# Fewer decode steps beside the attention, scans first, shared banks for weights and norms

## The chip, the cores and the metric

The kernel runs on one core of a Trainium2 chip. The metric is the time of one execution on the device in microseconds. Engines: PE (matmuls and weight loads), DVE (vector), ACT (activations), POOL (GpSimd), and SP, whose queue issues all the transfers spoken of here. PE, DVE, ACT and POOL run their instructions in the order in which the program lists them; SP issues its DMAs in program order too.

## The reference

One step of a two-layer decoder for a prompt of 1024 positions and for 8 sample rows with 4096 cached positions each, all float32, model width 1024.

Layer 0 projects the input to q, k, v, two gates and a pooling branch. Eight heads of 64 attend by stick breaking:

```
z = q.k / 8 + bias                       strictly causal
w[t,s] = sigmoid(z[t,s]) * prod over s<j<t of (1 - sigmoid(z[t,j]))
o = w v
```

For the sample rows the keys and values are paged: 32 pages of 128 keys a row, from a pool through a page table. Four groups of the pooling branch take window means. Both branches are gated, projected out, added to a scaled residual and layer-normed. Layer 1 is a convolution module: projection, sigmoid gate, depthwise convolution of 31 taps, layer norm over channels, SiLU, gate, output projection, residual, layer norm.

## The kernel before

A float32 matmul is made of three matmuls of split operands (high part, low part): `project` for the input projections and `out_group` for the output projections, 24 matmuls of 256 columns for a tile of 128 rows and a quarter of the outputs.

The order on PE, ACT, DVE and POOL is the order in which Python calls the engines. Work that is to run beside other work lies in generators: `Filler` advances projection blocks by parts, `tick(n)` advances the sample group's decode by n steps, and `defer`/`point` postpone a function by some points.

*Attention.* 48 units of at most 512 keys: four pairs of heads, eight query blocks, and for the last four blocks two units each, the nearer keys first. An iteration u calls `z_a(u)` (scores in two PSUM banks on PE, then four sigmoids on ACT), `ppart(u-2)` (weights times values on PE), parts of the projections, half of its ticks, `z_b(u)` (for each head a scan and a product on DVE, L365 to L371), more parts, `tpart(u-1)` (PE transposes the weights of both heads into PSUM, L845, ACT copies them to SBUF, L847), the rest of the ticks. How many ticks an iteration has is a running sum of TBASE plus a term in the number of keys. `trp()` hands out PSUM banks in turn, five in this stage, for scores, transposes and whatever else.

*K decode.* A step of `decode_k` loads a pair of pages (two DMAs of 256 KB on SP, L405, into one of four buffers), multiplies the pair that was loaded two steps ago by the query (L417, on POOL or, one time in KMOD, on DVE) and reduces the pair before that over the head dimension (L409 on DVE). Two halves of four rows have 64 pairs each; behind each half come transposes, sigmoids, a scan over the keys and products, in ten steps. Steps that are left when the attention ends run in the first output projection, one for each of its 32 groups, and in the first parts of the next stage.

*Output projections.* `out_layer` goes through 32 groups (four quarters, eight tiles of 128 rows). Behind each group DVE adds the residual (L1062) and takes statistics (L1066). When a tile has all quarters, `norm_s` makes mean and rs (DVE, POOL) and a deferred function applies the norm: a first pass on DVE, (y - mean) x gamma (L1009 with gamma in PSUM, in halves, L1013 with gamma in SBUF), a second one, y x rs + beta, on DVE for the tiles in FAST (L1018), else on ACT (L1020) and POOL (L1021). The first projection has gamma in two PSUM banks, the second not. In the second every other group's accumulator is a `trp()` bank, of which that stage has four.

*Between.* The convolution stage runs projections on PE, taps on DVE, ACT and POOL, the V decode and the sample path in ticks. Then `mid_a` spreads the norm's mean and rs of a chunk of tiles over partitions (transposes L1555, L1556, into a `trp()` bank of which that stage has two), `mid_b` applies them on DVE (L1567), and SiLU, gate and split follow, before the second output projection.

Of the kernel before, what the change touches and what calls it, by code (L numbers as in the profile page):

```python
# [14 lines left out]
F32 = mybir.dt.float32  # L15
# [3 lines left out]
AF = mybir.ActivationFunctionType  # L19
# [5 lines left out]
P = 128  # L25
D = 1024
S = 1024
# [18 lines left out]
KS = 30  # L46
PS_ = 15
NEG = -1e30
KMOD = 8
KPOOL = 7  # L50
ENG = mybir.EngineType
KLAG = 2
DTB = 2
# [12 lines left out]
WRB = 3  # L66
ETICK = 0.35
EDVE = (1, 2, 3, 0)
TBASE = 2.8
TSLOPE = 1.5  # L70
NHEADS = (0, 6, 6, 6, 6, 6, 6, 6)
SNY = 7
# [12 lines left out]
SNZ = 5  # L85
HALVES = (3, 6)
OLAG = 3
FAST = (5, 6, 7)
WCONVA = ((0, 5), (1, 5))
SY = 2  # L90
VRATE = 1.575
# [9 lines left out]
def kernel(  # L101
# [44 lines left out]
    def trp():  # L146
        return pz[0].tile([P, 512], F32, tag="zt", name="zt", bufs=NZT[0])
# [323 lines left out]
    def tick(n):  # L471
        while n > 0 and queue:
            try:
                next(queue[0])
                n -= 1
            except StopIteration:
                queue.pop(0)
# [359 lines left out]
    def tpart(u):  # L837
        pair, qb, c0, c1, first, last = units[u]
        n = c1 - c0
        wts = []  # L840
        for hh in range(2):
            w = st["w", u, hh]
            t = trp()
            for i in range(n // P):
                pe.transpose(out=t[:, i * P:(i + 1) * P], in_=w[:, i * P:(i + 1) * P], identity=ident)  # L845
            wt = ab.tile([P, 512], F32, tag="wt", name="wt", bufs=3)
            act.activation(out=wt[:, 0:n], in_=t[:, 0:n], func=AF.Copy)  # L847
            wts.append(wt)
        st["t", u] = wts
# [97 lines left out]
    for u in range(len(units) + 2):  # L947
        if u < len(units):
            pair, qb, c0, c1, first, last = units[u]
            n = c1 - c0  # L950
            if u % 12 == 0:
                fill.until(f"v{pair}")
                fleft = 42 if pair < 3 else 45
                fbase = fleft / 12.0
            fcred += fbase
            tcred += TBASE + TSLOPE * (384 - n) / 384.0
            z_a(u)
        k = int(tcred)
        tcred -= k
        f = min(int(fcred), fleft)  # L960
        fcred -= f
        fleft -= f
        fs = [(f + 2 - i) // 3 for i in range(3)]

        def slot(i):
            if i == PAT and u > 1:
                ppart(u - 2)
            if i == TAT and 0 < u <= len(units):
                tpart(u - 1)

        slot(0)
        fill.part(fs[0])
        tick((k + 1) // 2)
        if u < len(units):
            z_b(u)
        slot(1)
        fill.part(fs[1])
        slot(2)
        tick(k // 2)
        fill.part(fs[2])  # L980
        slot(3)
# [23 lines left out]
    def norm_a(gb, y, mv, halves, gps):  # L1005
        if gps:
            for i in range(2):
                h = slice(i * 512, i * 512 + 512)
                dve.scalar_tensor_tensor(out=y[:, h], in0=y[:, h], scalar=mv[:, 0:1], in1=gps[i],  # L1009
                                         op0=ALU.subtract, op1=ALU.mult)  # L1010
            return
        for h in halves:
            dve.scalar_tensor_tensor(out=y[:, h], in0=y[:, h], scalar=mv[:, 0:1], in1=gb[:, 0, h],  # L1013
                                     op0=ALU.subtract, op1=ALU.mult)

    def norm_b(gb, y, rs, fast, h):
        if fast:
# [15 lines left out]
    def out_layer(w, first, ahead, X, gb, pool, finish, between, before=None, half=None, tail=None, lag=OLAG, fast0=FAST, wide=0, gps=()):  # L1033
# [16 lines left out]
        for s, (n4, tb) in enumerate(order):  # L1050
# [16 lines left out]
            if n4 == 3:  # L1067
                fast = tb in fast0
                halves = (slice(0, 512), slice(512, 1024)) if tb >= 6 else (slice(0, 1024),)
                mv, rs = norm_s(pool, sts[tb])  # L1070

                def app(y=y, mv=mv, rs=rs, tb=tb, fast=fast, halves=halves):
                    norm_a(gb[0], y, mv, halves, gps)
                    for h in halves:
                        norm_b(gb[0], y, rs, fast, h)
                        finish(tb, y, h)
                defer((DTC if fast0 is FASTB else DTD)[tb], app)
# [472 lines left out]

    def mid_a(c):
        a, b = MID[c]
        t = trp()
        for i, tb in enumerate(range(a, b)):
            pe.transpose(out=t[:, i * P:(i + 1) * P], in_=rmf[:, tb:tb + 1].broadcast_to([P, P]), identity=ident)  # L1555
            pe.transpose(out=t[:, 256 + i * P:256 + (i + 1) * P], in_=rvf[:, tb:tb + 1].broadcast_to([P, P]),  # L1556
                         identity=ident)
        BC[c] = t
# [37 lines left out]
            X[tb] = C[:, tb].rearrange("p k c -> p (k c)")  # L1596
            sp.dma_start(X[tb], x1_dram[tb * P:(tb + 1) * P, :])

    gb1 = [None]

    def before(n4, tb):
        if (n4, tb) in STEPS:
            STEPS[n4, tb]()
        if n4:
            return
        if tb == 3:
            gb1[0] = G[:, 0:2].rearrange("p t k c -> p t (k c)")
            sp.dma_start(gb1[0][:, 0, :], ln_c_g.to_broadcast([P, D]))
            sp.dma_start(gb1[0][:, 1, :], ln_c_b.to_broadcast([P, D]))
# [22 lines left out]
    mid_c(0)  # L1632
    mid_g(1)
    flush()
    swap_psum("pzd", 4)
    cxp.close()
    dx = ctx.enter_context(tc.tile_pool(name="dx", bufs=1, reuse_waits="tile"))
    fill.part(2)
# [14 lines left out]
    mid_g(2)  # L1653
    flush()
    deep[0] = DEEPD
    out_layer(w_out1, first1, ahead1, X, gb1, dx, fin1, lambda n4, tb: tick(1), before, lambda: tick(1))
    while queue:
        tick(1)
    flush()
# [24 lines left out]
```

## Time and profile before

| | |
|---|---|
| median of 3 runs | 1143.98 us (1140.2 to 1145.24) |
| profiled execution | 1143.3 us, span 1141.5 us |
| granted clock, mean | 0.971 |
| PE busy | 1051.7 us, 92% |
| DVE busy | 812.6 us, 71% |
| POOL busy | 665.1 us, 58% |
| ACT busy | 491.9 us, 43% |

The page also cuts the span into 40 equal slices of 28.5 us; a digit is the busy share in tenths:

```profile
PE   8998888889999998797998999999999999899994
DVE  3458878688599898767348399999999960484246
POOL 3277879691788889872418336765766612343235
DMA  8577767783467976655203887787687678386922
```

The attention is about the fourth to the eighteenth slice, the first output projection the nineteenth to the twenty-second, the convolution stage follows up to the thirty-fourth, and the second output projection has the last five.

### The profile page before, as it was taken

The page shows a single profiled execution, that of the slowest core. Times are in us where ns is not written, and L with a number is a line of the kernel's source. Part 1 is how long each engine was busy: PE and PEld are TensorE (multiplying, and loading weights), DVE is VectorE, ACT ScalarE, POOL GpSimd, SP SyncE. Part 2 cuts the span into 40 slices and gives each one's busy share as a digit, 9 for nine tenths or more (in the row PEclk, how much of TensorE's full clock was granted, in tenths as well). Part 3 has the DMA queues.
Part 4 walks back from the last instruction along what each step waited for, and adds up shares of the span by engine and source line. Part 5 has one row for each costly group of instructions (what it writes and reads, how often), then busy time and mean ns, then how long its engine had stood idle before and what let it go on. Part 6 is the DMA issues. An engine that isn't in the chain of part 4 may idle for free.

```text
span 1141.5 us, 19830 instructions
## 1 busy us (share of the span) xinstructions
PE 1051.7 (92%) x6804; PEld 841.7 (74%) x6804; DVE 812.6 (71%) x961; ACT 491.9 (43%) x929; POOL 665.1 (58%) x502
## 2 busy tenths in 40 slices
PE   8998888889999998797998999999999999899994
PEld 7897777768877877697997666566666466677784
DVE  3458878688599898767348399999999960484246
ACT  4345465547565565571204224444544422462210
POOL 3277879691788889872418336765766612343235
PEclk9999999999999999898999999999999999899997
DMA  8577767783467976655203887787687678386922
GB/s 267 170 230 231 243 194 222 207 251 98 141 217 219 278 216 216 199 194 203 68 26 142 240 253 249 234 252 217 194 266 236 210 237 264 122 280 218 322 102 113
DMA packets 179206, 235.20 MB, mean 206 GB/s; under 512 B 15418, under 2 KB 95939, under 8 KB 179081
## 3 DMA queue, kind: packets, MB, share of 16 engines
q1 hardware_dynamic: 179105, 233.94, 65.1%
q8 instruction: 53, 0.87, 0.3%
q14 instruction: 48, 0.39, 0.1%
HBM read 212.60 MB, written 16.14 MB: 200 GB/s over the span
## 4 chain that ended last, share of the span: by engine, by line
PE 54%; POOL 13%; DVE 11%; issue 9%; DMA 7%; ACT 3%; SPq 3%; POOLq 0%; DVEq 0%; ACTq 0%
PE acc L225 11%; PE acc L227 10%; PE acc L226 10%; POOL kt L417 7%; PE qv L1151 5%; DMA kt<-in_cache_k_dram 3%; DVE zw L409 3%; PE acc L1029 3%; POOL wlo L210 2%; PE acc L1031 2%; PE acc L1030 2%; DVE kp L365 2%; DMA vt<-in_cache_v_dram 1%; DVE xl L196 1%; POOL xres L1021 1%
## 5 line engine op out<-in xcount | busy, mean ns | idle before, releaser
L225 PE MATMUL acc<-xh,whi 128*128 128x384 f32 (+2 forms) x960 | 361.5, 377 | 11.5 <-DVE hbt L705 5.7
L227 PE MATMUL acc<-xl,whi 128*128 128x384 f32 (+2 forms) x960 | 340.4, 355 | 0.2 <-DVE xl L196 0.2
L226 PE MATMUL acc<-xh,wlo 128*128 128x384 f32 (+2 forms) x960 | 339.7, 354 | 0.0
L417 POOL TENSOR_TENSOR kt<-kt,qbs 128x1024 f32<-128x1024 f32 x112 | 274.1, 2464 | 39.6 <-DMA kt<-in_cache_k_dram 30.0
L210 POOL TENSOR_TENSOR wlo<-wraw,whi 128x512 fp32r<-128x512 f32 x122 | 161.6, 1328 | 184.1 <-ACT whi L205 179.5
L1373 DVE SCALAR_TENSOR_TENSOR conv_acc<-hbuf,wdwT,conv_acc 128x1024 f32<-128x1024 f32 x196 | 252.8, 1290 | 6.8
L225 PEld LDWEIGHTS acc<-xh,whi 128*128 128x128 f32 x960 | 184.3, 192 | 78.1 <-issue 26.1
L409 DVE TENSOR_REDUCE zw<-kt 128x16 f32<-128x1024 f32 x128 | 153.6, 1212 | 63.5 <-POOL kt L417 63.3
L227 PEld LDWEIGHTS acc<-xl,whi 128*128 128x128 f32 x960 | 184.3, 192 | 18.0 <-DVE xl L196 0.7
L226 PEld LDWEIGHTS acc<-xh,wlo 128*128 128x128 f32 x960 | 185.0, 193 | 15.7 <-issue 0.3
L1363 POOL TENSOR_TENSOR conv<-conv,tap 128x512 f32<-128x512 f32 x84 | 105.9, 1293 | 17.6 <-ACT tap L1360 17.6
L1029 PE MATMUL acc<-whi,xh 128*128 128x256 f32 x352 | 102.4, 291 | 0.0
L1031 PE MATMUL acc<-whi,xl 128*128 128x256 f32 x352 | 99.5, 283 | 2.1 <-DVE xl L196 2.1
L1030 PE MATMUL acc<-wlo,xh 128*128 128x256 f32 x352 | 99.4, 282 | 0.0
L365 DVE TENSOR_TENSOR_SCAN kp<-kp,zt 128x512 f32<-128x512 f32 (+3 forms) x96 | 92.4, 963 | 1.2 <-ACT zt L361 1.2
L205 ACT ACTIVATE whi<-wraw 128x512 fp32r<-128x512 f32 x126 | 77.4, 624 | 32.1 <-DMA wraw<-in_w_out_ab_dram 14.1
L360 ACT ACTIVATE kp<-zt,nbiash 128x512 f32<-128x512 f32 (+3 forms) x96 | 55.8, 581 | 71.4 <-DVE sg L371 40.7
L1360 ACT ACTIVATE tap<-hbuf,wdwT 128x512 f32<-128x512 f32 x84 | 59.7, 721 | 48.0 <-POOL conv L1363 38.1
L1151 PE MATMUL qv<-vt,zw 128*32 128x512 f32 x512 | 76.1, 604 | 3.1 <-DMA vt<-in_cache_v_dram 3.1
L1029 PEld LDWEIGHTS acc<-whi,xh 128*128 128x128 f32 x352 | 66.8, 190 | 7.9 <-issue 7.4
L1031 PEld LDWEIGHTS acc<-whi,xl 128*128 128x128 f32 x352 | 67.0, 190 | 2.3 <-DVE xl L196 2.3
L845 PE MATMUL zt<-ident,sg 128*128 128x128 f32 x288 | 44.7, 286 | 24.2 <-DVE sg L371 12.9
(274 smaller groups left out, 1507.3 us busy)
## 6 DMA issues: line engine op xcount, KB each, us to landing
kt<-in_cache_k_dram SPq DMA_DIRECT2D x256, 256.0 KB
vt<-in_cache_v_dram SPq DMA_DIRECT2D x256, 256.0 KB
wraw<-in_w_in_c_dram SPq DMA_DIRECT2D x48, 256.0 KB
vt<-in_w_in_c_dram SPq DMA_DIRECT2D x48, 256.0 KB
wraw<-in_w_in_ab_dram SPq DMA_DIRECT2D x46, 256.0 KB
xt<-in_x_prompt_dram SPq DMA_DIRECT2D x8, 512.0 KB
wraw<-in_w_out_ab_dram SPq DMA_DIRECT2D x16, 256.0 KB
xres<-in_x_prompt_dram SPq DMA_DIRECT2D x8, 512.0 KB
```

What stands on the lines that cost most here:

```text
L210: (eng or gp).tensor_tensor(out=lo, in0=raw, in1=hi.bitcast(F32), op=ALU.subtract)
L225: pe.matmul(o, hi[:, k % 4, :], xh, start=(k == 0), stop=False)
L226: pe.matmul(o, lo[:, k % 4, :], xh, start=False, stop=False)
L227: pe.matmul(o, hi[:, k % 4, :], xl, start=False, stop=(k == NK - 1))
L365: dve.tensor_tensor_scan(out=kr, data0=kr, data1=z[:, 0:1].broadcast_to([P, n]), initial=1.0 if prev is None else prev, op0=ALU.mult, op1= ...
L409: dve.tensor_reduce(out=seg[:, j // 8, j % 8:j % 8 + 2, bi * 8:bi * 8 + 8], in_=kts.pop(s - KLAG - 1).rearrange("p a (h d) -> p a h d", d=DH),
L417: eng.tensor_tensor(out=kt, in0=kt, in1=qrow[b], op=ALU.mult)
L1029: pe.matmul(o, XH[:, k, cs], hi[:, k % 2, :], start=(k == 0), stop=False)
L1030: pe.matmul(o, XH[:, k, cs], lo[:, k % 2, :], start=False, stop=False)
L1031: pe.matmul(o, XL[:, k, cs], hi[:, k % 2, :], start=False, stop=(k == NK - 1))
L1151: pe.matmul(pv[32 * bi:32 * bi + 32, :], Z[:, j % 8 * 4 + j // 8, :], vts[bi], start=(j == 0), stop=(j == NPG - 1), tile_position=(0, 32 * ...
L1373: dve.scalar_tensor_tensor(out=part[1], in0=hb[:, j:j + S], scalar=w, in1=part[1], op0=ALU.mult, op1=ALU.add)
```

## The change

TBASE goes from 2.8 to 2.35, KMOD and KPOOL from 8 and 7 to 4 and 3, FAST loses tile 6. In the attention's loop `z_b(u)` is called ahead of the first ticks. Units of at most 256 keys put the transposes of both heads into one bank and copy them at once. A fast tile in a layer that has gamma in PSUM takes `norm_fast`: the first pass writes into a `trp()` bank, the second reads it; the second projection now gets gamma in PSUM too. That layer's `trp()` banks go from four to three. `mid_a` puts the first two chunks into the bank pair that held the convolution's accumulator.

```
-KMOD = 8
-KPOOL = 7
+KMOD = 4
+KPOOL = 3
-TBASE = 2.8
+TBASE = 2.35
-FAST = (5, 6, 7)
+FAST = (5, 7)
 def tpart(u):
+        if n <= 256:
+            t = trp()
+            for hh in range(2):
+                for i in range(n // P):
+                    pe.transpose(out=t[:, hh * 256 + i * P:hh * 256 + (i + 1) * P],
+                                 in_=st["w", u, hh][:, i * P:(i + 1) * P], identity=ident)
+            wt = ab.tile([P, 512], F32, tag="wt", name="wt", bufs=3).rearrange("p (a n) -> p a n", a=2)
+            act.activation(out=wt[:, :, 0:n], in_=t.rearrange("p (a n) -> p a n", a=2)[:, :, 0:n], func=AF.Copy)
+            st["t", u] = [wt[:, 0], wt[:, 1]]
+            return
...
         fill.part(fs[0])
-        tick((k + 1) // 2)
         if u < len(units):
             z_b(u)
+        tick((k + 1) // 2)
...
+    def norm_fast(gb, y, mv, rs, h, i, gps):
+        t = trp()
+        dve.scalar_tensor_tensor(out=t, in0=y[:, h], scalar=mv[:, 0:1], in1=gps[i], op0=ALU.subtract, op1=ALU.mult)
+        return lambda: dve.scalar_tensor_tensor(out=y[:, h], in0=t, scalar=rs, in1=gb[:, 1, h], op0=ALU.mult, op1=ALU.add)
...
+                    if fast and gps:
+                        hs = (slice(0, 512), slice(512, 1024))
+                        bs = [norm_fast(gb[0], y, mv, rs, h, i, gps) for i, h in enumerate(hs)]
+                        for h, b in zip(hs, bs):
+                            b()
+                            finish(tb, y, h)
+                        return
...
 def mid_a(c):
-        t = trp()
+        if c == 0:
+            BC["wide"] = pz[0].tile([P, S], F32, tag="conv", name="rows", bufs=1)
+        t = BC["wide"][:, c * 512:c * 512 + 512] if c < 2 else trp()
...
+        if (n4, tb) == (2, 4):
+            gps1.extend((psum("o", 1), pg.tile([P, 512], F32, name="scale1")))
+            for i in range(2):
+                act.activation(out=gps1[i], in_=gb1[0][:, 0, i * 512:i * 512 + 512], func=AF.Copy)
...
-    swap_psum("pzd", 4)
+    swap_psum("pzd", 3)
+    pg = ctx.enter_context(tc.tile_pool(name="pg", bufs=1, space=PSUM, reuse_waits="tile"))
```

## Rows read from the trace of the kernel before

**Rows 1.** Stretches: busy us (count) of PE, PEld, DVE, ACT, POOL; PEclk, DMA share, GB/s
```profile
80.00:503.00 423.00, 376.92 (x2576) 326.73 (x2575) 336.68 (x408) 236.34 (x490) 328.43 (x182) 0.96 0.68 210
...
536.00:588.00 52.00, 52.00 (x441) 51.83 (x440) 18.64 (x39) 7.83 (x16) 11.99 (x11) 1.00 0.14 42
588.00:640.00 52.00, 47.80 (x329) 41.81 (x327) 32.54 (x59) 20.39 (x32) 33.43 (x45) 1.00 0.44 147
...
1127.00:1141.50 14.50, 0.21 (x2) 0.01 (x1) 9.85 (x15) 0.85 (x1) 6.84 (x6) 0.61 0.37 145
```

**Rows 2.** Waits of PE, 80 to 503 us: us in total, times, longest
```profile
PE zt L845 <- DVE sg L371: 12.9, 7, 3.2
PE zt L845 <- DVE sg L369: 10.8, 10, 2.4
PE acc L225 <- DVE hbt L705: 5.7, 4, 2.3
```

**Rows 3.** Waits of DVE, 80 to 503 us
```profile
DVE zw L409 <- POOL kt L417: 57.1, 31, 5.4
...
DVE kp L365 <- ACT zt L361: 1.2, 1, 1.2
```

**Rows 4.** Timeline of DVE: start us, us, instruction, [idle before <-releaser]
```profile
227.72 1.22 DVE L409 TENSOR_REDUCE zw<-kt 128x16 f32<-128x1024 f32 x1 [2.63 <-POOL kt L417]
...
231.20 1.27 DVE L365 TENSOR_TENSOR_SCAN kp<-kp,zt 128x512 f32<-128x512 f32 x1
```

**Rows 5.** Timeline of PE, the same stretch
```profile
233.39 0.66 PE L845 MATMUL zt<-ident,sg 128*128 128x128 f32 x4 [2.60 <-DVE sg L371]
```

**Rows 6.** DVE by form, 80 to 503 us: busy us, mean ns, idle before
```profile
L409 DVE TENSOR_REDUCE zw<-kt 128x16 f32<-128x1024 f32 x118 | 141.7, 1212 | 57.4 <-POOL kt L417 57.1
...
L417 DVE TENSOR_TENSOR kt<-kt,qbs 128x1024 f32<-128x1024 f32 x15 | 26.9, 1792 | 0.0
...
L437 DVE TENSOR_TENSOR_SCAN kpd<-kpd 128x1024 f32<-128x1024 f32 x1 | 2.3, 2279 | 0.0
```

**Rows 7.** POOL by form, 80 to 503 us
```profile
L417 POOL TENSOR_TENSOR kt<-kt,qbs 128x1024 f32<-128x1024 f32 x104 | 254.4, 2464 | 39.3 <-DMA kt<-in_cache_k_dram 29.7 <-DVE kp L365 3.9 <-DVE zw L409 3.2
L210 POOL TENSOR_TENSOR wlo<-wraw,whi 128x512 fp32r<-128x512 f32 x43 | 56.6, 1318 | 26.7 <-ACT whi L205 26.7
```

**Rows 8.** Line 417, the whole span: ns min/median/max, first and last start us
```profile
L417 DVE TENSOR_TENSOR kt<-kt,qbs x16: 1209/1276/3224, 79.5 to 524.8; 128x1024 f32<-128x1024 f32 x16
```

**Rows 9.** ACT by form, 80 to 503 us
```profile
L847 ACT ACTIVATE wt<-zt 128x512 f32<-128x512 f32 x48 | 26.4, 601 | 14.9 <-PE zt L845 14.8
...
L847 ACT ACTIVATE wt<-zt 128x256 f32<-128x256 f32 x16 | 5.4, 385 | 2.6 <-PE zt L845 2.6
```

**Rows 10.** Timeline of DVE in the first output projection, one group
```profile
564.42 0.42 DVE L1062 SCALAR_TENSOR_TENSOR xres<-xres,acc 128x256 f32<-128x256 f32 x1 [1.96 <-PE acc L1031]
564.88 0.43 DVE L1066 BATCH_NORM_STATS2 st<-xres 128x6 f32<-128x256 f32 x1
```

**Rows 11.** Timelines of PE and of POOL before the second output projection
```profile
987.79 0.45 PE L1555 MATMUL zt<-ident,rmu 128*128 128x128 f32 x1 [5.68 <-DVE conv L1567]
...
993.26 0.69 POOL L1243 COPY sB<-shs 128x64 f32<-128x64 f32 x1
```

**Rows 12.** Timeline of DVE at the end
```profile
1122.67 3.58 DVE L1013 SCALAR_TENSOR_TENSOR conv<-conv,mv,gate 128x1024 f32<-128x1024 f32 x2
1127.53 1.28 DVE L1018 SCALAR_TENSOR_TENSOR conv<-conv,rs,gate 128x1024 f32<-128x1024 f32 x1 [1.29 <-POOL rs L1002]
...
1129.94 2.29 DVE L1013 SCALAR_TENSOR_TENSOR conv<-conv,mv,gate 128x512 f32<-128x512 f32 x2
...
1137.09 1.41 DVE L1018 SCALAR_TENSOR_TENSOR conv<-conv,rs,gate 128x512 f32<-128x512 f32 x2 [0.45 <-POOL rs L1002]
```

**Rows 13.** Groups by line over the whole span, with gamma in PSUM
```profile
L1009 DVE SCALAR_TENSOR_TENSOR xres<-xres,mv,qv 128x512 f32<-128x512 f32 x8 | 5.9, 740 | 0.0
...
L1018 DVE SCALAR_TENSOR_TENSOR xres<-xres,rs,lngb 128x512 f32<-128x512 f32 x2 | 3.2, 1626 | 0.0
```

**Rows 14.** Chain of waits: start us, us, what
```profile
150.35 4.79 DMA kt<-in_cache_k_dram
```

More of the change, by code (lines that the diff above doesn't have):

```diff
@@ L1597, in mid_c @@
             sp.dma_start(X[tb], x1_dram[tb * P:(tb + 1) * P, :])
-    gb1 = [None]
+    gb1, gps1 = [None], []
     def before(n4, tb):
@@ L1655 @@
     deep[0] = DEEPD
-    out_layer(w_out1, first1, ahead1, X, gb1, dx, fin1, lambda n4, tb: tick(1), before, lambda: tick(1))
+    out_layer(w_out1, first1, ahead1, X, gb1, dx, fin1, lambda n4, tb: tick(1), before, lambda: tick(1), gps=gps1)
     while queue:
```

## The prediction, before the run

> **What bounds the kernel now.** I read the table of stretches first [rows 1]: its PE column says where the tensor engine stands idle and its clock column where it runs at 1.2 instead of 2.4 GHz. Of the 1141.5 us span, 80 to 503 us is the attention loop with the K pages of the sample group decoded beside it. PE is busy there for 376.9 of 423 us, 46 us idle, and the granted clock averages 0.96. The output projection after it (536 to 588 us) has PE busy throughout while DVE works 18.6 and POOL 12.0 of 52 us, and DMA moves only 42 GB/s. So the idle tensor time is in the attention, and the spare vector, POOL and DMA time lies right behind it.
>
> Who keeps PE waiting is in the waits of PE [rows 2]: transposes of the attention weights (L845) that wait for the last vector step of those weights (12.9 and 10.8 us), and projection groups that wait for DVE to empty an accumulator (5.7 us). Always DVE. What DVE itself waits for is POOL: 57.1 us before the page reduction L409, against 1.2 us for the sigmoids its scans need [rows 3]. One stretch of DVE's timeline shows the mechanism [rows 4]: a reduction waits 2.63 us for POOL's product, and the scan of the next weights comes only behind it and another reduction; PE's transposes of those weights then start after 2.60 us of idling [rows 5]. DVE runs in order, so a wait for POOL is a wait of everything behind it. Busy time plus waits for POOL is 336.7 + 57.1 = 394 of DVE's 423 us: with its waits DVE, not PE, sets the pace here. POOL in turn is busy for 328.4 us and waits some 30 us for pages and 27 us for weights [rows 7].
>
> **The change part by part.** The sum is made against the profiled execution, 1143.3 us (span plus 1.8), which is 0.7 us under the median of the runs.
>
> *Fewer K steps in the attention (TBASE 2.8 to 2.35).* Counted from the code: the loop over 48 units issues 48 x TBASE steps of the K decode (the term in n sums to zero), 134 before and 112 after, behind 8 steps issued earlier. The decode has 155. So 13 steps are left for the projection before, 35 after: 22 pages' pairs (two DMAs, one product, one reduction each) leave the attention. *Products three of four on POOL instead of seven of eight (KMOD, KPOOL).* Up to the end of the attention DVE now makes 26 of 104 products instead of 15 of 126, POOL 78 instead of 111.
>
> DVE in the attention: 22 reductions less at 1.212 us, -26.7; 11 products more at 1.792 us, +19.7 [rows 6]; busy 336.7 - 7.0 = 329.7 us. POOL: 33 products less at 2.464 us, -81 us, 328 to 247 [rows 7]. What remains of DVE's 57.1 us of waits for POOL no row shows. Below it is 0 (POOL has 40% of its time free), above 57.1 (nothing changes). I take half, 28.5: the lateness that comes from POOL's own load should go, that which comes from the landing of pages stays, since the rate of page loads per us hardly changes. DVE's other idle time, 423 - 336.7 - 57.1 = 29.2, I keep. 329.7 + 28.5 + 29.2 = 387.4: -36 us. The ends: with all waits kept 416, -7; with none kept 359, and then PE is the bound: by the clock column some 34 of its 423 us ran at half speed, which at full speed would take 17 less of its 376.9 busy us, so 360, -63.
>
> A price for DVE's product that speaks against this stands in its own row: 1.209 us at least, 1.276 in the median, 3.224 at most [rows 8]. At 3.224 us for all 26 the attention gains 37 us less: 26 x 3.224 - 26.9 is +57 instead of +19.7; at 1.276 it gains 13 more. I stay at the mean, which holds both kinds. The Trainium skill, GPSIMD Engine Reference, section Key points, says that POOL shares its SBUF interfaces with VectorE and contends with DVE instructions that have two SBUF inputs. These products have two, so by that rule the long price is to be expected whenever POOL works beside them, and the attention would gain next to nothing. The trace agrees in part: rows 8 have the long price, but half of the products took 1.276 us or less while POOL was busy for 328 of 423 us.
>
> *Scans ahead of the steps.* Nothing is added or removed; z_b moves past one or two steps of each iteration, and past nothing on SP or POOL. The weights are then ready before DVE can be caught behind POOL. What it adds is the wait of a scan for PE and the sigmoids of the same iteration, with the reductions queued behind it, and behind those SP's page loads that wait for free buffers. In rows 3 that wait is 1.2 us in all because DVE is late; it only grows when DVE is early, when it costs nothing. I count it inside the 28.5 us.
>
> *One bank and one copy for units of up to 256 keys.* 16 of 48 units. In half of them two copies of 385 ns become one like the 601 ns form [rows 9], 0.17 us less; the smaller half saves as much: 16 x 0.17 = 2.7 us on ACT, which is busy for 236 of 423 us [rows 1]. Both heads now wait for the later one, but the products that read them come an iteration later. Zero, at most +1; the freed bank may take a little off too.
>
> *The 22 pairs in the output projection.* A group there takes 2.84 us: DVE's 0.42 and 0.43, then 1.96 us idle for PE [rows 10]. A step adds 1.212 + 1.792/4 = 1.66, so DVE has 2.5 of 2.84 us (2.87 with every product at 3.224). POOL gets 0.75 x 2.464 = 1.85 us a group, and 3.15 in the eight groups with a 1.318 us weight split, 2.5 us too much in all; pages are requested three groups before their reduction. DMA goes from 42 to some 210 GB/s, what the attention has [rows 1]. Hidden in the main, but the residual rows and weights are loaded on the same SP queue: I take +4, from 0 to +12 (half a microsecond a group). Behind it the end of the decode, with a scan of 2.279 us on DVE [rows 6], falls into the normalisation (588 to 640 us, DVE 32.5 of 52 busy): +2, 0 to +5. The last tile's two second passes there took 1.626 us each; like the first ones with a PSUM operand they should take about 0.74 [rows 13]: 1.8 us less, of which I count -1, 0 to -2.
>
> *Broadcast rows of the convolution's norm in a bank of their own.* PE waits 5.68 us here [rows 11] because the third broadcast needs the bank of the second, which DVE reads late. That wait goes. But the next thing on PE after two parts of a projection is the sample product, and its operand is copied on POOL at 993.26 [rows 11], behind work that hangs on the same DVE chain and not on this bank. PE would be there as much earlier and wait. 0, from -6 to +1; the one bank fewer for the last projection I price within it.
>
> *The tail.* PE ends at about 1127 us [rows 1], and DVE works off norms until 1138.5, the end of the last row [rows 12]. A step of 1024 takes 1.28 us there, but two others take 3.58; two halves take 1.41 or 2.29. With gamma in PSUM a half costs 0.74 [rows 13], so a tile's first pass is 1.48. Tiles 5 and 7 go through four such steps, tile 6 gives its second pass (1.41 us) to ACT and POOL, and the waits of 1.29 us for rs shrink since DVE no longer sits on it between. Laid out from 1122.67: tile 4's first pass ends at 1124.2, tile 5's at 1125.6 and its second at 1127.1, instead of 1128.8. Tile 6 adds its last sum and statistics (1.15) and a first pass: 1129.8. The same for tile 7: 1132.4. Its rs comes on POOL behind tile 6's two halves of 1.2, which start at 1130.5 behind ACT's 0.6: 1132.9, and 0.8 for rs. The second pass then ends at 1135.2 instead of 1138.5. -3, from -5 (no wait for rs) to +1 (POOL's halves as much stretched as DVE's).
>
> Sum: -36 + 4 + 2 - 1 + 0 - 3 = -34 us: 1109.
>
> **Rivals.**
> *The waits for POOL stay (1130).* POOL's products wait for pages 29.7 us [rows 7], and steps still come in pairs, so a reduction asks for a product issued just before it. Then the attention gains its 7 us of work and a few of the order, say 15, and with the other terms 1143.3 - 15 + 4 + 1 - 3 = 1130. For it: DMA is at 0.68 share before and after. Against it: pages are three steps ahead, and 81 us of POOL work go.
>
> *PE becomes the bound (1085).* Scans first and a POOL at under two thirds leave nothing late; attention -58 (5 above its floor), the rest as above: 1143.3 - 58 + 2 - 2 = 1085. For it: all four large waits in rows 2 are behind DVE. Against: DVE would have to be busy for 330 of 365 us without catching on anything.
>
> *The projection gives it back (1157).* Place: groups 0 to 23 of the first output projection. A page buffer comes free with a reduction on DVE and is used again four units on; between lie the landing, POOL's product behind a weight split, and the reduction: 2.46 + 1.32 + 1.21 = 5.0 us plus the landing, for four groups. A slow landing took 4.79 us [rows 14], so 9.8 us for four groups, 2.45 each, under the 2.84 of PE. If residuals, weights and pages together bring the landing to 15 us, a group takes 5.0 us, 24 of them cost 52 us more, and the sum is 1109 - 4 + 52 = 1157. It begins to cost from a landing of 6.4 us and eats all (38 us) from 12.7. Against it: some 210 GB/s are asked, which the attention has all the time.
>
> *It does not do what it says (1145).* DVE is as late as before, since its own work falls by 7 us only and products at the long price of rows 8 eat that and the shorter waits: -36 + 37 in the attention, + 4 + 1 - 3 behind it: 1146, or 1145 with one of them short. POOL is then faster and nobody gains by it. The page named at rows 8 stands for this one.
>
> **How the numbers follow.** Forecast 1109 (0.60, own range 1094 to 1122); waits stay 1130 (0.17); PE the bound 1085 (0.11); gives it back 1157 (0.05); nothing 1145 (0.07). The range 1086 to 1136 leaves out the two cases at the top and half of the lowest. Under 0.5%, 5.7 us, a change of this kernel can't be told from none. Faster by more: 0.60 + 0.17 + 0.11 = 0.88; within: 0.07; slower: 0.05.
>
> **What would show it.** Right: between the start and the end of the attention PE idles for under 25 us, DVE's waits for POOL before L409 fall to around 28 us and come behind the scans, L845's waits for DVE fall from 23 us to a few; L409 and L417 run on into the normalisation, with projection groups still 2.84 us apart; PE idle before L1555 is gone and stands before the sample product; the last DVE step comes 3 us sooner after the last matmul. Wrong: groups over 3 us apart with DVE waiting for POOL; DVE's products mostly at 3 us; PE in the attention idle as long as before.

## The result, and the profile after

The changed kernel takes 1112.17 us (median of 4 runs, 1107.29 to 1117.8) against 1144.59 us of the kernel before in the same comparison: ratio 0.9726, 95% interval 0.9673 to 0.978, faster. The forecast was 1109. The execution that was profiled took 1107.29 us, of which 1105.5 are the span. Its span is 36.0 us shorter than that of the profile before, near the forecast's 34, but the gain does not lie in the same places.

The busy times of the page after:

```profile
PE 1040.4 (94%) x6804; PEld 837.7 (76%) x6804; DVE 830.9 (75%) x982; ACT 493.1 (45%) x917; POOL 628.8 (57%) x488
```

The table of stretches after, with the columns of [rows 1]: the attention, the middle of the first output projection, its end with the start of the convolution stage, and the tail:

```profile
80.00:465.00 385.00, 370.00 (x2611) 326.75 (x2611) 329.36 (x402) 238.71 (x482) 259.38 (x153) 0.98 0.68 206
...
493.00:545.00 52.00, 46.90 (x392) 46.28 (x391) 40.81 (x53) 6.06 (x10) 41.14 (x21) 1.00 0.75 247
545.00:608.00 63.00, 53.27 (x352) 47.28 (x354) 38.96 (x66) 24.63 (x39) 36.01 (x50) 0.95 0.35 122
...
1095.00:1105.50 10.50, 0.00 (x0) 0.00 (x0) 6.05 (x12) 1.33 (x2) 5.15 (x7) 0.64 0.52 201
```

PE idles 15 us in the attention, where it idled 46. In the first projection's middle DVE and POOL, which had most of that time free before, are busy for 41 of 52 us, and PE, which had been busy throughout, now idles 5. The third line is new trouble: PE idles 10 of 63 us there.

To see where time is won and lost, the same instructions are looked up in PE's timeline of each trace. Times in us, and the lead that a kernel has over the kernel before at that point:

```
                                      before   after   lead   lead:    lead:   lead: decode earlier
                                                              steps    order   and norm in SBUF
                                                              alone    alone   (see below)
first matmul, first out-projection     507.2   465.7   41.5    38.4     13.8    40.5
last matmul of that projection         614.7   576.4   38.3    25.3     14.0    33.0
last transposes of its normalised rows 632.0   600.7   31.3    17.8     14.1    31.3
PE's last matmul                      1127.2  1094.7   32.5    16.6     13.5    32.8
end of the span                       1141.5  1105.5   36.0    16.7     13.1    36.3
```

(Of the kernel after the fastest execution was profiled, of the steps alone the slowest of four and of the last column's kernel the slowest of five, so that the first and the last column of leads end alike where the medians differ by 8 us; and one execution of the order alone, the 1141.57 us below, fell into a slower state and is not in its ratio.) The attention wins 41.5 us (36 forecast), the projection and the start of the convolution stage give back 10.2 (5 forecast), 1.2 more come up to PE's last matmul, and the tail wins 3.5 (3 forecast).

The two longest waits of PE in the attention after, columns as in [rows 2]:

```profile
PE zt L713 <- DVE hbt L705: 3.7, 1, 3.7
PE zt L815 <- issue: 2.8, 2, 1.7
```

The two large waits of [rows 2], the transposes of the weights behind DVE's last weight steps, were 23.7 us and are not among these. And what DVE waits for, beside [rows 3]:

```profile
DVE zw L409 <- POOL kt L417: 18.3, 16, 3.7
DVE qo L756 <- ACT sga_t L754: 8.9, 1, 8.9
DVE kp L365 <- ACT zt L361: 6.1, 5, 2.5
```

57.1 us of waits for POOL are 18.3 now, and the scans' wait for the sigmoids grew from 1.2 to 6.1 us, as the prediction said that it would when DVE is early. The 8.9 us before L756, a step of the setup, were as long before.

### The profile page after: what moved, and what is told of

Read it like the earlier page. It is cut to its first block, busy times and chain, and to the rows that moved or that the text cites. A ratio compares the mean times of both kernels' runs of the same rounds, so it can differ in the third digit from the quotient of the medians.

```text
span 1105.5 us, 19839 instructions
## 1 busy us (share of the span) xinstructions
PE 1040.4 (94%) x6804; PEld 837.7 (76%) x6804; DVE 830.9 (75%) x982; ACT 493.1 (45%) x917; POOL 628.8 (57%) x488
## 4 chain that ended last, share of the span: by engine, by line
PE 52%; DVE 8%; DMA 5%; POOL 4%; ACT 3%; issue 2%; SPq 1%; POOLq 0%; DVEq 0%; ACTq 0%
PE acc L225 11%; PE acc L227 10%; PE acc L226 10%; PE qv L1173 6%; DMA kt<-in_cache_k_dram 2%; DVE conv L1591 2%; POOL kt L417 2%; PE acc L1044 2%; PE zt L1044 1%; PE qv L1209 1%; PE o L871 1%; PE acc L1046 1%; PE acc L1045 1%; PE zt L1046 1%; PE zt L1045 1%
## 5 line engine op out<-in xcount | busy, mean ns | idle before, releaser
L417 POOL TENSOR_TENSOR kt<-kt,qbs 128x1024 f32<-128x1024 f32 x96 | 235.7, 2466 | 77.0 <-DMA kt<-in_cache_k_dram 61.7
L1045 PEld LDWEIGHTS acc<-wlo,xh 128*128 128x128 f32 x352 | 67.2, 191 | 1.1 <-POOL wlo L210 1.1
```

The lines of the kernel that those rows point to most:

```text
L417: eng.tensor_tensor(out=kt, in0=kt, in1=qrow[b], op=ALU.mult)
L1045: pe.matmul(o, XH[:, k, cs], lo[:, k % 2, :], start=False, stop=False)
```

## The experiments

Each experiment has its own median and a ratio to the kernel before, run on the same chip in turns with it. The kernel before had medians of 1142.56, 1140.9 and 1143.89 us in the three sets (the first four experiments, the next four, the last four), and the kernel after ran in a set of its own: between sets the ratios compare better than the medians.

**The parts of the attention alone.** Two theories: *W*, that the fewer steps bring the gain, as in the prediction's sum; *O*, that the order of scans and steps does. Four kernels: the kernel before with one part each, and the kernel after with one part taken back.

```diff
-TBASE = 2.8
+TBASE = 2.35
```

> The kernel before with TBASE 2.35 alone: 22 pairs of pages leave the attention, order and shares stay. Theory W (the work on DVE and its waits for POOL set the pace of the attention): DVE does 22 reductions and 3 products less, 336.7 - 32 = 305 us, waits for POOL half of 57, so PE is the bound and the attention is 40 to 45 us shorter; 10 to 15 us are given back up to the convolution stage, where the decode now ends; no gain at the tail: about 1144 - 42 + 13 = 1115. Theory O (the order scans behind steps makes PE wait, and the order alone cures it): attention at most 10 us shorter, the same given back: 1144 to 1150.

Measured: 1120.08 us (1118.25 to 1126.64), ratio 0.9801 (0.9773 to 0.9829).

```diff
-        tick((k + 1) // 2)
         if u < len(units):
             z_b(u)
+        tick((k + 1) // 2)
```

> The kernel before with z_b ahead of the first steps and nothing else. Theory W: DVE has the same work and waits for POOL, so it is as late as before: attention 0 to 8 us shorter, 1136 to 1144. Theory O: the scans no longer stand behind reductions that wait for POOL, the 23 us that L845 waits for DVE go and part of the rest: 1112 to 1120.

Measured: 1129.79 us (1123.09 to 1141.57), ratio 0.986 (0.9817 to 0.9904).

```diff
-KMOD = 8
-KPOOL = 7
+KMOD = 4
+KPOOL = 3
```

> The kernel before with three of four products on POOL instead of seven of eight and nothing else. Theory W: DVE takes 16 more products in the attention, +29 us at 1.79, POOL loses 39 us, DVE's waits for POOL fall by about 29: 1140 to 1148. Rival P (POOL alone is the bound, DVE's waits follow its load at once): waits fall from 57 to under 15 and DVE's products are short: 1125 to 1132. Theory O: no change, 1144.

Measured: 1151.28 us (1149.63 to 1153.27), ratio 1.0083 (1.0056 to 1.011).

The fourth is the kernel after with the order of before (the second diff backwards):

> The changed kernel with z_b again behind the first steps. Theory W: the order is worth little once DVE has time left: 0 to 6 us over the changed kernel, 1112 to 1118. Theory O: the 23 us come back: 1132 to 1138.

Measured: 1117.88 us (1116.68 to 1120.07), ratio 0.9787 (0.976 to 0.9814).

The same stretch of each, 80 to 460 us, and DVE's waits for POOL in it. The kernel before:

```profile
80.00:460.00 380.00, 341.44 (x2335) 295.46 (x2335) 309.05 (x377) 212.99 (x451) 294.38 (x165) 0.97 0.69 211
DVE zw L409 <- POOL kt L417: 51.1, 28, 5.4
```

Fewer steps alone:

```profile
80.00:460.00 380.00, 360.68 (x2550) 314.96 (x2549) 304.97 (x383) 233.74 (x487) 275.05 (x160) 0.99 0.67 205
DVE zw L409 <- POOL kt L417: 40.6, 24, 3.4
```

The order alone:

```profile
80.00:460.00 380.00, 345.71 (x2374) 300.97 (x2373) 318.60 (x388) 215.58 (x456) 299.24 (x167) 0.97 0.71 216
DVE zw L409 <- POOL kt L417: 36.1, 31, 5.5
```

The share alone:

```profile
80.00:460.00 380.00, 337.84 (x2279) 292.00 (x2277) 327.24 (x388) 206.76 (x441) 261.87 (x148) 0.95 0.69 208
DVE zw L409 <- POOL kt L417: 32.4, 20, 5.4
```

The kernel after with the order of before:

```profile
80.00:460.00 380.00, 359.70 (x2545) 313.31 (x2544) 321.99 (x398) 232.80 (x470) 251.38 (x147) 0.99 0.68 206
```

The numbers in brackets behind PE count its matmuls: how far a kernel gets in the same time. With fewer steps 2550, with the share alone 2279. Fewer steps make the attention 38 us shorter, just under W's 40 to 45; 21 us of that are lost again behind it in the profiled execution (the table of leads), and by the medians the whole is 22 us shorter. The order alone makes the attention 14 us shorter and loses nothing, which is more than W allowed and half of what O asked. What it takes away is seen in the waits; PE's for DVE with the order alone:

```profile
PE acc L225 <- DVE hbt L705: 7.9, 5, 2.6
PE acc L225 <- DVE kl L611: 6.0, 2, 3.3
PE zt L845 <- DVE sg L371: 5.2, 6, 1.4
```

L845's waits, 22.5 us in this stretch of the kernel before, fall to 5.4 with as many steps as before; DVE still waits 36.1 us for POOL, and projections still wait for the accumulator (13.9 us, 11.2 before). In the kernel after the order is worth 5.7 us by the medians and 7 by the ratios, with intervals that overlap; its attention is 4 us longer without it, longer than in any of the six profiled runs that have the attention of the kernel after. So the order and the steps take away the same waits, and their gains don't add: 38 and 14 alone, 41.5 together.

The share alone costs 8.7 us: DVE gets 18 us of work more, and its waits for POOL fall by 18.7, so that DVE is as late as before and L845's waits stay (22.7 us). I had expected a loss of at most half of 8.7 us.

Two sums can be held against PE's idle time in these 380 us. By the waits for POOL alone, the kernels would stand in another order: 51.1 us in the kernel before, 40.6 with fewer steps, 36.1 with the order, 32.4 with the share, where PE idles 38.6, 19.3, 34.3 and 42.2 us. DVE's busy time plus these waits is 360.2, 345.6, 354.7 and 359.6 us: it sets fewer steps first and the order second, as PE's idle time does, and leaves the kernel before and the share alone last and alike.

**The share taken back in the kernel after.**

```diff
-KMOD = 4
-KPOOL = 3
+KMOD = 8
+KPOOL = 7
```

> The kernel after with POOL making 7 of 8 products again instead of 3 of 4. About 14 products of the attention go from DVE (1.6 us each, 22 us less on DVE) to POOL (2.45 us each, 34 us more, 290 of 385). Theory S (DVE's busy time sets the attention once the steps are fewer, as the share alone cost 9 us in the kernel before): DVE's waits for POOL grow by less than 12 us and the attention is 5 to 10 us shorter, 1102 to 1107. Theory P (the share and the fewer steps are needed together, POOL's lateness comes back): DVE's waits for POOL grow by over 22 us and it takes 1115 to 1125.

Measured: 1111.53 us (1109.89 to 1116.37), ratio 0.9741 (0.9713 to 0.9768). It is the same time, between what the two theories asked; the waits grew by less than 12 us, as S had it, but nothing was gained by it. The stretch of the attention, beside the first line of the table after:

```profile
80.00:465.00 385.00, 371.30 (x2610) 328.85 (x2610) 306.49 (x388) 238.32 (x482) 282.03 (x164) 0.97 0.67 205
```

DVE has 23 us less to do and POOL 23 more, and PE stands where it stood, busy for 371 instead of 370 of 385 us. DVE's waits for POOL are 24.5 us instead of 18.3, and its waits for ACT's copies grow (L794 from 4.7 to 8.6 us, L611 to 6.4). With 2.35 steps a unit, neither the work of DVE nor that of POOL sets the attention's end any more; PE is within 14 us of it. The share, which was one of the sum's terms (+19.7 us on DVE), is worth nothing in the kernel after.

**One bank and one copy taken back.**

```diff
-        if n <= 256:
+        if False:
```

> The kernel after with each head's transposed weights in a bank and a copy of its own again, also for units of at most 256 keys. ACT gets about 2.7 us of copies back in the attention, of 236 busy in 385 us. If ACT and the banks have slack, as the prediction has it: within 2 us of the kernel after, 1110 to 1114. If the bank that the shared copy saves is what lets PE run ahead: PE waits for zt banks grow and the attention is 5 to 10 us longer, 1117 to 1122.

Measured: 1112.42 us (1104.34 to 1116.16), ratio 0.9744 (0.9713 to 0.9776). No difference, as the sum had it.

**The tail taken back.**

```diff
-FAST = (5, 7)
+FAST = (5, 6, 7)
...
-        if (n4, tb) == (2, 4):
-            gps1.extend((psum("o", 1), pg.tile([P, 512], F32, name="scale1")))
-            for i in range(2):
-                act.activation(out=gps1[i], in_=gb1[0][:, 0, i * 512:i * 512 + 512], func=AF.Copy)
...
-    swap_psum("pzd", 3)
+    swap_psum("pzd", 4)
```

(and the last projection called without gamma's copies)

> The kernel after with the last normalisation of before: gamma from SBUF, tile 6 on the fast path, four banks instead of three in the last projection. If the tail's gain is what the rows at the end show: the span's last part is 3 to 4 us longer and nothing else moves, 1115 to 1116. If the bank given up costs as much in the last projection as the norm gains: 1111 to 1113, with the projection's last matmul earlier.

Measured: 1114.81 us (1114.48 to 1117.91), ratio 0.9772 (0.9745 to 0.9798). From PE's last matmul to the end of the span it takes 14.3 us, as before the change; the kernel after takes 10.8. The last projection itself is as long with four banks as with three (127.7 and 128.4 us from its first matmul to its last). The intervals of the whole overlap; the 3.5 us rest on the traces alone.

**Where the gain is given back.** Between the last projection group and the last transposes of the normalised rows the kernel after loses 7.0 us. PE's timeline of the kernel after there; in square brackets the idle time before the instruction:

```profile
582.79 0.23 PE L451 MATMUL zt<-ident,crow 1*128 1x1 f32 x1 [2.49 <-DVE xl L196]
...
585.68 1.19 PE L1148 MATMUL zt<-ident,xres 128*128 128x128 f32 x8
589.60 1.97 PE L463 MATMUL zt<-ident,zw 128*128 128x128 f32 x8 [2.73 <-DVE xl L196]
```

and DVE's, up to the step that released PE at 589.60:

```profile
583.88 0.75 DVE L1028 SCALAR_TENSOR_TENSOR zt<-xres,mv,o 128x512 f32<-128x512 f32 x1
584.53 0.75 DVE L1028 SCALAR_TENSOR_TENSOR zt<-xres,mv,qv 128x512 f32<-128x512 f32 x1
585.30 1.41 DVE L1029 SCALAR_TENSOR_TENSOR xres<-zt,rs,lngb 128x512 f32<-128x512 f32 x2
586.63 2.20 DVE L454 SCALAR_TENSOR_TENSOR zw<-kpd,car,zw 128x1023 f32<-128x1023 f32 x1
588.75 0.20 DVE L456 TENSOR_SCALAR zw<-zw,car 128x1 f32<-128x1 f32 x1
588.88 1.27 DVE L196 TENSOR_TENSOR xl<-zt,xh 128x512 fp32r<-128x512 f32 x2
```

Three users want the zt banks (those of `trp()`) here: the transposes of the normalised rows (L1148), the decode's last transposes (L451, L463), and, new with this change, the last tile's first pass, which writes two of these banks (L1028) and gives them back only with L1029. What PE waits for in this run is the decode: L451 for a bank, L463 first for its operand, which the scan L454 and L456 make behind L1029 and have ready at 588.95, and then 0.65 us more for a bank. For the norm's banks it does not wait here: the transposes at 585.68 begin before the first half of L1029 is over. PE's eight transposes at 589.60 take 1.97 us, where eight like them take 1.06 elsewhere (below): behind the two stalls the granted clock is low. The 14 us from 582 have PE busy for 10.48 at a mean granted clock of 0.76.

*Theory D*: the decode's end, which 35 instead of 13 steps in the projection push into the convolution stage, costs it. So two steps a group in the last seven groups:

```diff
-              lambda n4, tb: tick(1), before0, None, tail0, OLAGB, FASTB, WIDE, gps0)
+              lambda n4, tb: tick(2 if n4 == 3 and tb > 0 else 1), before0, None, tail0, OLAGB, FASTB, WIDE, gps0)
```

> The kernel after, with two steps of the decode instead of one behind each of the last seven groups of the first output projection, so that the decode ends ahead of the convolution stage. Theory D (the decode's last transposes take the convolution stage's two transpose banks and stall PE, whose clock then falls): the 7 us that the start of the convolution stage lost come back, the last eight projection groups lose up to 2: 1104 to 1107. Rival R (the moved pages' work in the projection is what costs, wherever it stands): the loss moves into the last groups and the time stays within 2 us, 1110 to 1114.

Measured: 1109.59 us (1106.44 to 1111.78), ratio 0.9711 (0.9685 to 0.9737): between the two expectations, so its time decides nothing. Its trace does. PE's timeline:

```profile
576.76 1.06 PE L463 MATMUL zt<-ident,zw 128*128 128x128 f32 x8 [0.73 <-DVE zw L456]
...
592.11 1.94 PE L1148 MATMUL zt<-ident,xres 128*128 128x128 f32 x8 [5.25 <-DVE xres L1029]
```

The decode is out of the way 13 us sooner, and another wait has taken its place: transposes of rows that POOL had ready at 588.8, behind L1029, the step that frees the last tile's banks. *Theory B*: the banks that the norm holds are a cause of their own, which shows once the decode is out of the way. So the last tile of this layer is normalised in SBUF as before, first without and then with the earlier decode:

```diff
-                    if fast and gps:
+                    if fast and gps and gps is not gps0:
```

> The kernel after with the first layer's last tile normalised as before, in SBUF: its two first passes no longer take the two transpose banks of the convolution stage. The decode's end stays where it is. Theory B (the banks that the norm holds and the decode's last transposes stall PE at the same place, and each alone is enough): 0 to 3 us less, 1109 to 1112. Rival N (the passes in SBUF cost DVE more there than the banks cost PE): 1 to 3 us more, 1113 to 1115.

Measured: 1112.14 us (1111.01 to 1115.41), ratio 0.9742 (0.972 to 0.9765): no gain alone. PE's wait before L463 has grown:

```profile
594.48 1.97 PE L463 MATMUL zt<-ident,zw 128*128 128x128 f32 x8 [5.70 <-DVE xl L196]
```

The second pass in SBUF (L1033) takes DVE 3.42 us for its two halves, where L1029 takes 1.41, and the decode's scan stands behind it: that is rival N's mechanism, at this place.

> Both: the decode's end two steps a group in the last seven groups, and the last tile normalised in SBUF. Theory B: the 5.25 us wait of PE for the norm's bank at the start of the convolution stage goes, and the stretch of lower clock behind it (6.8 us at 1.2 GHz, so some 3 us); with the earlier decode, 1102 to 1106. Rival N: no gain over the earlier decode alone, 1108 to 1112.

Measured: 1104.5 us (1102.86 to 1106.97), ratio 0.9667 (0.9647 to 0.9687), faster than the kernel after by 8 us by the medians and 7 by the ratios. Its interval lies clear of that of the bank alone and touches that of the kernel after (from 0.9673). PE's timeline with both:

```profile
577.48 1.06 PE L463 MATMUL zt<-ident,zw 128*128 128x128 f32 x8 [0.72 <-DVE zw L456]
...
589.56 1.69 PE L1148 MATMUL zt<-ident,xres 128*128 128x128 f32 x8 [1.97 <-POOL xres L1036]
```

From the last projection group to the last row's transposes it now takes 19.0 us, 1.7 more than before the change, where the kernel after takes 24.3, the earlier decode alone 22.5, and the norm in SBUF alone 26.7. Each mend alone brings little (2.6 us by the medians, and none), since with one of them the other's wait is there or grows, and both together 8. This kernel is the fastest of all that ran.

**The broadcast bank taken back.**

```diff
-        if c == 0:
-            BC["wide"] = pz[0].tile([P, S], F32, tag="conv", name="rows", bufs=1)
-        t = BC["wide"][:, c * 512:c * 512 + 512] if c < 2 else trp()
+        t = trp()
```

> The kernel after with the broadcast rows of the convolution's norm in the transpose banks again. The prediction put the bank's change at nothing: 1110 to 1114, with PE's wait of 5 us before the third broadcast as long as in the kernel after. Rival: the first two broadcasts, which now run 5 us earlier, let DVE start earlier; then 3 to 6 us more, 1115 to 1118.

Measured: 1111.22 us (1107.81 to 1118.89), ratio 0.9738 (0.9709 to 0.9767): nothing. The kernel after in PE's timeline, beside [rows 11]:

```profile
948.91 0.27 PE L1579 MATMUL zt<-ident,rmu 128*128 128x128 f32 x1
...
954.75 0.45 PE L1579 MATMUL zt<-ident,rmu 128*128 128x128 f32 x1 [5.24 <-DVE conv L1591]
```

The third broadcast's transposes run without a wait now (948.91), and the fourth's wait, for the same step of DVE: 5.24 us instead of 5.68. With the old banks in the kernel after it is the fifth's that wait, for that step again:

```profile
958.94 0.45 PE L1577 MATMUL zt<-ident,rmu 128*128 128x128 f32 x1 [4.80 <-DVE conv L1589]
```

So the third's freedom is not the bank's doing. The kernel with fewer steps alone, which has the old banks too, waits before none of these transposes, but then here, before the sample product:

```profile
PE qv L1187 <- POOL sB L1243: 7.8, 1, 7.8
```

Which broadcast meets a bank that DVE has yet to read differs from kernel to kernel, and no run shows by what.

**A few steps given back to the attention.** On top of both mends:

```diff
-TBASE = 2.35
+TBASE = 2.5
```

> As the kernel with both, with 2.5 instead of 2.35 decode steps a unit in the attention: 7 pages fewer are left for the output projection. By what the steps alone brought (38 us for 22 pages, 1.75 each, against 13 us given back in the projection, 0.6 each), the attention is 12 us longer and the projection 4 shorter: 1110 to 1114. If the attention has nothing left to gain from fewer steps, since PE idles there only 15 us, and the projection is what the pages cost: 1099 to 1104.

Measured: 1118.28 us (1113.58 to 1119.34), ratio 0.9774 (0.9751 to 0.9797), 14 us more than with 2.35. The attention is 13.5 us longer (12 expected), and the projection up to the last transposes of its rows 4.5 us shorter (4 expected). The profiled span is 11.5 us longer, so 2.5 us are lost behind that point; the median lies above the expected 1114, the fastest run within. The stretch again:

```profile
80.00:465.00 385.00, 358.45 (x2511) 313.97 (x2511) 335.43 (x404) 229.15 (x463) 263.97 (x150) 0.98 0.68 207
```

PE idles 26.5 instead of 15 us of 385, and its waits for DVE in the projections are back (7.8 us behind L611, 6.1 behind L705). A pair of pages costs 1.9 us in the attention and 0.6 in the projection.

## Why the prediction was right, and where not

*The total.* It came out near the forecast partly by luck: the attention won 5.5 us more than forecast, and the projection with what follows it gave back 5.2 us more.

*The bound.* Right in its form: DVE, by its work together with its waits for POOL, set the pace. The experiments with one part each bear that sum out, and not the waits for POOL alone. Of the 41.5 us that the attention won, 31 are idle time of PE; the other 10 are PE's busy time, 381 us up to the projection's first matmul before and 371 after for as many matmuls, at a granted clock of 0.96 before and 0.98 after. The prediction had the clock only in the case in which PE is the bound.

*DVE's sum in the attention.* Busy time was put at 329.7 us and is 329.36 in 385. That it was met so well is partly luck: the products cost 5 us less than priced, and 4 us of splits (L196), which lay behind the window of [rows 6], fall into this one. Waits for POOL were put at 28.5, halfway between bounds, and are 18.3. The 29.2 us of other idle time, kept in the sum, are 37; the largest growth is that of the scans' wait for the sigmoids, from 1.2 to 6.1. The sum came to 387.4 us; the attention ended 41.5 us earlier instead of 36. That two terms were off by 8 to 10 us in opposite directions is why it looks better than its parts. The products' price, to see beside [rows 6]; DVE by form in the attention after:

```profile
L409 DVE TENSOR_REDUCE zw<-kt 128x16 f32<-128x1024 f32 x98 | 116.7, 1212 | 20.2 <-POOL kt L417 18.3 <-DMA out_dram<-vrow 1.5
L417 DVE TENSOR_TENSOR kt<-kt,qbs 128x1024 f32<-128x1024 f32 x25 | 39.8, 1592 | 0.0
```

The mean of 1.79 us was taken and 1.59 measured; 15 of the 25 took under 1.25 us, nine took 1.7 us or more. The Trainium skill, GPSIMD Engine Reference, section Key points, says that POOL shares its SBUF interfaces with VectorE and contends with DVE instructions that have two SBUF inputs: the trace agrees that such a price exists (up to 3.5 us, and 2.4 us in the mean of the four products between 493 and 545 us, where POOL is busy for 41 of 52), but most products in the attention didn't pay it. Laid beside POOL's timeline, the nine that took 1.7 us or more had POOL busy for 0.38 of their time or more; of the 15 under 1.25 us ten had it busy for under a fifth, and five for 0.7 or more. So the price came only with POOL at work, but not each time. And the run with the share taken back shows that the term is worth nothing in the kernel after at either price.

*The parts' worth.* The order was counted inside the waits, with no term of its own. Alone it brings 13 us: the reading of [rows 4] and [rows 5], that weights stand behind a reduction that waits for POOL, was right, and should have been carried into the sum by itself.

*One bank and one copy.* Zero forecast, nothing measured.

*Pages in the output projection.* +4 forecast, from 0 to 12; 3.2 us in the profiled run, and 4.8, 6.6, 7.2 and 9.4 in the four kernels that have the same projection (two copies, old tail, old broadcast, norm in SBUF). The cover that was named held for three quarters of the stretch: behind 24 groups the lead is what it was at the first matmul to within 1.4 us in four of these five kernels (4.2 us with the norm in SBUF), though DVE is busy for 41 of 52 us. The groups' distance was to stay 2.84 us; from group 8 to group 24 it is 3.2 in the profiled run, which had gained 5 us in the first eight groups (its PE waits 2.0 us for a weight split on DVE there, the other four 6.0), and 2.9 to 3.1 in the others, where the kernel before has 2.9. Over 3 us with DVE waiting for POOL (6.8 us in the profiled run's projection) was among the prediction's signs of being wrong. The loss stands in the last eight groups, 3.5 to 6.6 us, where PE waits for rows that are normalised late (before L1148; 3.5 us in the kernel after, 1.2 in the kernel before). POOL's last pass on them waits for ACT, and in the way stand the decode's reductions on DVE up to 550.5 and its sigmoids on ACT (L433, L434), from 560.8 to 564.5:

```profile
PE acc L1044 <- DVE xres L1077: 4.5, 2, 2.4
PE zt L1148 <- POOL xres L1036: 4.4, 3, 1.9
PE zt L1045 <- DVE wlo L210: 3.6, 2, 2.0
PE zt L463 <- DVE xl L196: 2.7, 1, 2.7
PE zt L451 <- DVE xl L196: 2.5, 1, 2.5
```

These are PE's waits in the kernel after from 465 to 610 us, with the decode's two at the end.

*The decode's end and the last tile.* This is the step that failed: +2 and -1 forecast, +7.0 measured. The decode's scan was priced as time of DVE, and it is only 2.2 us; what was left out is that PE itself stands behind the decode's end: 2.5 us for a bank (L451), 2.7 us before L463, most of it for the scan, which stands behind the norm's passes on DVE, and that PE then runs at a low clock. The price of 0.74 us for a pass with gamma in PSUM was right (0.75); its output's banks were not counted at all, and they stall PE for 5.25 us once the decode ends sooner. Both mends together leave +1.7.

*The broadcast bank.* Zero was right, the reason was not seen at work: in the kernel after the wait stayed on the transposes (5.24 us), of a later broadcast, and 0.8 us stand before the sample product. That a wait which goes from the transposes comes back before the sample product, as the prediction had it, is seen in the kernel with fewer steps alone (7.8 us).

*The tail.* -3 forecast, -3.5 measured, and laid out the same. The end of DVE's timeline after, beside [rows 12]:

```profile
1098.43 0.75 DVE L1028 SCALAR_TENSOR_TENSOR zt<-conv,mv,o 128x512 f32<-128x512 f32 x1
1099.10 0.75 DVE L1028 SCALAR_TENSOR_TENSOR zt<-conv,mv,scale 128x512 f32<-128x512 f32 x1
1101.18 1.41 DVE L1029 SCALAR_TENSOR_TENSOR conv<-zt,rs,gate 128x512 f32<-128x512 f32 x2 [1.34 <-POOL rs L1012]
```

The first passes cost 0.75 us where 0.74 was taken. The last second pass waits 1.34 us for rs, where it waited 0.45 before [rows 12], as the layout of the prediction had it, and still starts 3.4 us sooner after PE's last matmul.

*The rivals.* Waits for POOL staying is out (18.3 us). The projection giving all back is out: a part is given back, but of 10 us, and not in the groups up to the 24th, where that rival placed it. PE as the bound came half true: PE idles 15 us of the attention, and taking 23 us off DVE changes nothing. That nothing is gained is out: most of DVE's products in the attention took the short price. What holds the last 15 us of PE's idle time stays open: POOL waits 48 us for pages there (30 before), DVE 18 for POOL, and no run told them apart.

## What to carry to other kernels

An engine that runs in order turns a wait for one producer into a wait of everything queued behind it: count its waits with its busy time, and look first at which item stands behind the waiting one. Putting that item ahead, or issuing less of the waiting kind in that stretch, took away the same time here, so the two gains didn't add. Work that is moved to an emptier stage arrives there with its own end: follow its last instructions and every buffer ring that they share, not only its cost per step. And where undoing one stall shows nothing, look in the trace for the wait that took its place, and undo both before calling either harmless.

## What the runs showed of the hardware that was not expected

Behind each of two idle stretches of 2.5 and 2.7 us within 10 us the granted clock fell to the lower of its two levels (1.2 instead of 2.4 GHz): PE's matmuls of 512 columns took 0.63 us instead of 0.39 behind the first, and its eight transposes 1.97 us instead of 1.06 behind the second. So the stalls cost more than their idling. By the mean granted clock of 0.76 over 14 us, PE was at half speed for some 6.8 us of them, which is an estimate of 3.4 us lost beside 5.2 us of idling. The row from 582 to 596 us:

```profile
582.00:596.00 14.00, 10.48 (x41) 8.68 (x42) 8.12 (x12) 4.19 (x8) 11.44 (x23) 0.76 0.64 212
```

The same DVE product on the same shapes, in the kernel after, took from 1.21 to 3.50 us within one execution (median 1.22 of 32):

```profile
L417 DVE TENSOR_TENSOR kt<-kt,qbs x32: 1207/1216/3496, 68.1 to 547.4; 128x1024 f32<-128x1024 f32 x32
```
